# Seven block products for eight in a second place, and weight blocks loaded in twos

## The chip, the core and the metric

The kernel runs on one core of a Trainium2 chip. Its engines are TensorE (PE, matmuls), VectorE (DVE), ScalarE (ACT), GpSimd (POOL) and SyncE (SP); all work in order from their own queues and wait for one another by semaphores. SP issues nearly all DMAs, POOL the accumulating ones. The metric is device time in microseconds (us) of one execution, the median over the runs; 1468.02 us before (three runs, 1467.19 to 1469.15).

## The reference

A trunk of two layers for 512 tokens and 16 learned ones ahead of them (528 in all), 1024 features, all float32. Layer 0 is forgetting attention, layer 1 a gated linear recurrence (HGRN2); each is followed by a gated MLP with a causal depthwise convolution of three taps:

```python
def conv_ffn(h, norm_g, w_gate, w_up, conv_w, conv_b, w_down):
    xn = rms_norm(h, norm_g)
    a = xn @ w_gate
    L = a.shape[1]
    a_pad = jnp.pad(a, ((0, 0), (CONV_WIDTH - 1, 0), (0, 0)))
    a = (conv_b + conv_w[0] * a_pad[:, 0:L] + conv_w[1] * a_pad[:, 1:L + 1]
         + conv_w[2] * a_pad[:, 2:L + 2])
    return (jax.nn.silu(a) * (xn @ w_up)) @ w_down
```

The hidden width is 2816, that is 22 tiles of 128. The change is in the two MLPs and in what feeds them.

## The kernel before

Features lie on the partitions, tokens along the free dimension. Each product is made from three matmuls of rounded float32: a block is split into hi (its rounded value, a cast on ScalarE) and lo (the rest, a subtraction on VectorE), and hi·hi, hi·lo and lo·hi are summed in PSUM. So `weights` (L183) loads a raw block by SP, casts hi, subtracts lo; it has two raw, three hi and three lo buffers of 128 x 1024 (512 KB).

An MLP (`ffn`) goes through its 22 hidden tiles in runs. `RUNS = [(0, 6), (12, 5)]` names a run's first tile and r, its number of pairs. For each tile `hidden` multiplies gate and up weights with the tokens: 8 input blocks x 3 matmuls for each half or all of the tokens (layer 0: two halves of 264 for both; layer 1: 256 and 258 for the gate, 512 for up). VectorE and ScalarE do the convolution, the silu and the product in between.

The down-projection is done after each run, for two output tiles at a time (four pairs of output tiles, `mp`): a matrix of 2 x 2 blocks (two output tiles by two halves of the run) times one of 2 x 2 blocks (two halves of the run by two halves of the tokens), by Strassen's scheme in Winograd's form, seven block products of r blocks each instead of eight. Its left sides are three blocks of the weights themselves (w11, w12, w22) and four sums s1 to s4 of blocks. The right sides, seven "forms", are made on VectorE from each pair of hidden tiles and kept in `fhi` and `flo`. Four PSUM banks A, B, C, D take the products; two copies on ScalarE hand a partial sum on, and `put` adds results to the residual `h`.

The sums s1 to s4 are made in DRAM ahead of time by `sum_blocks`, a generator: a step is an SP copy into a DRAM tile and one or two accumulating DMAs of POOL. One step is taken behind most weight loads (`next(self.summing, None)`): those of layer 0 from the attention's output projection on, those of layer 1 during HGRN2. The seven left sides of a down-projection are loaded by `left` (L1128), seven transfers of 384 or 320 KB, into a pool of eight buffers (`temp`) which the hidden tiles use too, and split by `parts` (L1117) in the same three hi and lo buffers.

A scheduler in the build sets the order of each engine's instructions from the program's dependences and its own estimate of durations; the text's order does not bind it. The order of the loads on SP and of the products on TensorE near the down-projection is therefore shown with the change.

Of the kernel before, what the change touches and what calls it, by code (L numbers as in the profile page):

```python
# [21 lines left out]
P = 128  # L22
# [7 lines left out]
RUNS = [(0, 6), (12, 5)]  # L30
# [51 lines left out]
class Builder:  # L82
# [97 lines left out]
    def weights(self, src, n, w=P, parts=1):  # L180
# [13 lines left out]
        if parts == 1:  # L194
            self.load = nc.sync.dma_start(raw, src)
            next(self.summing, None)
            nc.scalar.copy(hi, raw)  # L197
            self.sub(lo, raw, hi.bitcast(F32))
            return u
# [3 lines left out]
    def sum_blocks(self, layer):  # L203

        nc = self.nc
        for mp, c0, r in [(mp, *run) for run in RUNS for mp in range(KT // 2)]:
            src = lambda m, half: self.a[f"dn{layer}"][2 * mp + m][:, (c0 + half * r) * P : (c0 + half * r + r) * P]
            s1, s2, s3, s4 = self.sums[layer, mp, c0] = [
                self.hbm.tile([P, r * P], F32, name=f"s{i}", tag=f"s{i}_{layer}_{mp}_{c0}") for i in range(1, 5)
            ]  # L210
            w11, w12, w21, w22 = src(0, 0), src(0, 1), src(1, 0), src(1, 1)
            for out, x, *rest in (s1, w21, w22), (s2, w21, w22, w11), (s3, w11, w21), (s4, w12, s2):
                self.after(nc.sync.dma_start(out, x), self.load)
                for y in rest:
                    nc.gpsimd.dma_start(out, y, accum_op=ALU.add, max_dma_last_dim=4 * r * P)  # L215
                yield 1
# [127 lines left out]
    def fox(self, ctx):  # L344
# [320 lines left out]
        self.summing = self.sum_blocks(0)  # L665
# [117 lines left out]
    def hgrn(self, ctx):  # L783
# [239 lines left out]
        for m in range(-3, KT):  # L1023
            if m == -2:
                self.summing = self.sum_blocks(1)
# [20 lines left out]
    def ffn(self, ctx, layer, a0, o0):  # L1046

        nc, a = self.nc, self.a
        ga, up = (halves(t0) if T - t0 > 512 else [(t0, T - t0)] for t0 in (a0, o0))
# [3 lines left out]
        self.normsplit(gcol, a0)  # L1053
        segs = (SEG0, SEG1)[layer]
        am, rs = self.token_stats(segs)
        self.spread_rs(rs, segs)
        def unit(w, toks, x):
            for t0, tn in toks:
                ps = self.anybank()[:, :tn]
# [4 lines left out]
        n = T - o0  # L1064
        hw = n // 2

        def hidden(m, early=None):

            A, t, s = (temp(w, nm) for w, nm in ((T + 2, "A"), (n, "t"), (n, "s")))
            if o0 == 0:  # L1070
                nc.gpsimd.memset(A[:, 0:2], 0.0)
            wg, wu = (self.weights(a[f"gu{layer}"][m, i], KT) for i in range(2))
            if early is not None:
                early()
            for ps, t0, tn in unit([wg], ga, self.x):
                nc.vector.tensor_tensor(A[:, 2 + t0 : 2 + t0 + tn], ps, self.rsb[:, t0 : t0 + tn], ALU.mult)
            c0 = cw + 3 * m
# [5 lines left out]
            self.act(s, t, AF.Silu)  # L1083
            nc.vector.tensor_tensor(t, s, self.rsb[:, o0:], ALU.mult)
            for ps, t0, tn in unit([wu], up, self.x):
                tv = t[:, t0 - o0 : t0 - o0 + tn]
                nc.vector.tensor_tensor(tv, ps, tv, ALU.mult)
            return t
# [4 lines left out]
        def put_form(f, j, x, fhi, flo):  # L1093
            x = x.rearrange("p (f t) -> p f t", t=hw)
            f = slice(f, f + x.shape[1])
            nc.scalar.copy(fhi[:, f, j, :], x)
            self.sub(flo[:, f, j, :], x, fhi[:, f, j, :].bitcast(F32))
# [194 lines left out]
```

## Time and profile before

| | |
|---|---|
| median of three runs | 1468.02 us (1467.19 to 1469.15) |
| the profiled execution | 1466.04 us, of it a span of 1464.3 us |
| TensorE busy | 1442.8 us (99%), granted clock 0.998 |
| VectorE, ScalarE busy | 961.5 us (66%), 627.8 us (43%) |
| bytes moved | 202.64 MB, mean 138 GB/s |
| first down-projections: layer 0, layer 1 | from about 529.8 us, from about 1235.7 us |

A row of the timeline gives start, duration, engine, line, operation, tiles and shape, and in brackets the idle time before it with what ended it. "SPq" and "PEq" are the sequencers. A row of windows gives, for a stretch, the busy time of each engine with its count of instructions, the granted clock, the share of the 16 DMA engines and GB/s; with one engine chosen, that engine alone. A row of waits gives total, count and longest. Matmuls overlap in the pipeline: their price is the distance of starts.

### The profile page before, as it was taken

To read this page: it belongs to the slowest core of one execution; us is meant where nothing else is said; L and a number is where in the kernel's file an instruction comes from. 1 tells how busy PE (TensorE), PEld (TensorE's weight loads), DVE (VectorE), ACT (ScalarE), POOL (GpSimd) and SP (SyncE) were. 2 spreads that over 40 slices of the span, in tenths; PEclk is the share of its full clock that TensorE was granted. 3 is DMA by queue.
4 is the path that set the end of the run, shared out by engine and by line. 5 is a ranking of instruction groups with operands and counts; after the bars stand their busy time and mean duration, and the time that the engine had idled before them with its cause. 6 is when DMAs were issued, how large, how long until landed. Compare 5 with 4: busy or idle time off the path is not lost.

```text
span 1464.3 us, 29095 instructions
## 1 busy us (share of the span) xinstructions
PE 1442.8 (99%) x11620; PEld 1358.6 (93%) x11620; DVE 961.5 (66%) x2083; ACT 627.8 (43%) x1206; POOL 101.3 (7%) x205
## 2 busy tenths in 40 slices
PE   7999999999999999999999999999999999999999
PEld 6888888988999999999999999999999998999999
DVE  7555555775567765667776667687566666657665
ACT  5355555663344344334562333333343334434343
POOL 6000000001112200000001101111000000000000
PEclk9999999999999999999999999999999999999999
DMA  4433335436989973322636827475532234622254
GB/s 160 119 105 90 94 99 129 124 87 166 288 213 239 231 214 115 101 88 102 191 94 159 213 62 188 137 174 132 129 102 87 87 101 155 191 76 98 94 166 137
DMA packets 75934, 202.64 MB, mean 138 GB/s; under 512 B 10888, under 2 KB 13448, under 8 KB 75800
## 3 DMA queue, kind: packets, MB, share of 16 engines
q1 hardware_dynamic: 64280, 171.95, 36.9%
q0 software_dynamic: 11520, 28.84, 12.3%
q8 instruction: 91, 1.49, 0.4%
q14 instruction: 43, 0.35, 0.1%
HBM read 185.31 MB, written 54.00 MB: 163 GB/s over the span
## 4 chain that ended last, share of the span: by engine, by line
PE 95%; DMA 1%; DVE 1%; ACT 1%; issue 1%; SPq 1%; DVEq 0%; ACTq 0%
PE psp L226 12%; PE psp L229 12%; PE psp L230 12%; PE pss L230 8%; PE pss L226 8%; PE pss L229 8%; PE psp L275 6%; PE psp L1151 3%; PE psp L1149 3%; PE psp L1150 3%; PE psc L760 2%; PE psd L1150 1%; PE psd L1151 1%; PE psd L1149 1%; PE pss L914 1%; PE pss L689 1%
## 5 line engine op out<-in xcount | busy, mean ns | idle before, releaser
L226 PE MATMUL psp<-xhi,hi 128*128 128x264 f32 (+3 forms) x1160 | 352.1, 304 | 5.9 <-ACT xhi L295 5.9
L229 PE MATMUL psp<-xlo,hi 128*128 128x264 f32 (+3 forms) x1160 | 352.8, 304 | 2.8 <-DVE xlo L296 2.8
L230 PE MATMUL psp<-xhi,lo 128*128 128x264 f32 (+3 forms) x1160 | 352.7, 304 | 0.0
L197 ACT CAST hi<-raw 128x1024 fp32r<-128x1024 f32 (+1 forms) x170 | 174.8, 1029 | 317.7 <-PE psp L229 114.9
L125 DVE TENSOR_TENSOR lo<-raw,hi 128x1024 fp32r<-128x1024 f32 (+1 forms) x174 | 208.4, 1199 | 75.2 <-ACT hi L197 71.4
L226 PEld LDWEIGHTS psp<-xhi,hi 128*128 128x128 f32 x1160 | 218.7, 189 | 17.4 <-ACT xhi L295 5.9
L230 PE MATMUL pss<-xhi,lo 128*128 128x264 f32 (+2 forms) x824 | 233.7, 284 | 0.0
L226 PE MATMUL pss<-xhi,hi 128*128 128x264 f32 (+2 forms) x824 | 233.1, 283 | 0.0
L229 PE MATMUL pss<-xlo,hi 128*128 128x264 f32 (+2 forms) x824 | 233.0, 283 | 0.0
L229 PEld LDWEIGHTS psp<-xlo,hi 128*128 128x128 f32 x1160 | 219.3, 189 | 13.2 <-DVE xlo L296 3.8
L230 PEld LDWEIGHTS psp<-xhi,lo 128*128 128x128 f32 x1160 | 219.5, 189 | 9.4 <-issue 1.6
L226 PEld LDWEIGHTS pss<-xhi,hi 128*128 128x128 f32 x824 | 155.3, 189 | 0.9
L229 PEld LDWEIGHTS pss<-xlo,hi 128*128 128x128 f32 x824 | 155.1, 188 | 0.9
L230 PEld LDWEIGHTS pss<-xhi,lo 128*128 128x128 f32 x824 | 154.9, 188 | 0.0
L1122 ACT CAST hi<-left 128x768 fp32r<-128x768 f32 (+1 forms) x112 | 86.8, 780 | 113.3 <-PE psp L1150 41.0
L125 DVE TENSOR_TENSOR lo<-left,hi 128x768 fp32r<-128x768 f32 (+1 forms) x112 | 99.2, 891 | 44.5 <-ACT hi L1122 44.3
L1149 PE MATMUL psp<-fhi,hi 128*128 128x264 f32 (+1 forms) x352 | 99.8, 284 | 0.1
L1151 PE MATMUL psp<-fhi,lo 128*128 128x264 f32 (+1 forms) x352 | 99.5, 283 | 0.0
L1150 PE MATMUL psp<-flo,hi 128*128 128x264 f32 (+1 forms) x352 | 99.4, 282 | 0.0
L215 POOL DMA_DIRECT2D s<-dn x64 | 54.0, 871 | 285.3 <-DMA s<-dn 264.5
L118 ACT ACTIVATE s<-t 128x528 f32<-128x528 f32 (+1 forms) x44 | 28.1, 639 | 98.8 <-DVE t L1082 98.8
L275 PE MATMUL psp<-hi,xhi 128*128 128x256 f32 x232 | 66.9, 288 | 2.7 <-ACT v L562 2.7
(423 smaller groups left out, 3023.2 us busy)
## 6 DMA issues: line engine op xcount, KB each, us to landing
raw<-gu SPq DMA_DIRECT2D x88, 512.0 KB
pk<-stg SPq DMA_DIRECT2D x48, 264.0 KB
s<-dn SPq DMA_DIRECT2D x32, 384.0 KB
s<-dn POOLq DMA_DIRECT2D x32, 384.0 KB, 7.0
left<-s SPq DMA_DIRECT2D x32, 384.0 KB
s<-dn SPq DMA_DIRECT2D x32, 320.0 KB
s<-dn POOLq DMA_DIRECT2D x32, 320.0 KB, 6.5
left<-s SPq DMA_DIRECT2D x32, 320.0 KB
```

What stands on the lines that cost most here:

```text
L125: self.nc.vector.tensor_tensor(out, x, y, ALU.subtract)
L197: nc.scalar.copy(hi, raw)
L215: nc.gpsimd.dma_start(out, y, accum_op=ALU.add, max_dma_last_dim=4 * r * P)
L226: ins = mm(ps, hi[:, i, :], xh, start=k == 0, stop=False)
L229: mm(ps, hi[:, i, :], xl, start=False, stop=False)
L230: mm(ps, lo[:, i, :], xh, start=False, stop=k == total - 1)
L275: mm(ps[:tn, :256], y[:, t0 : t0 + tn], w, start=n == 0, stop=n == 23)
L760: ins = mm(o, v[:kn, j, 2 * (p % 2) + hd, :], w[hd][0], start=j == 0, stop=j == last)
L1122: nc.scalar.copy(hi, raw)
L1149: mm(ps, hi[:, c], xh, start=start and k == 0, stop=False, skip_group_check=not start)
L1150: mm(ps, hi[:, c], xl, start=False, stop=False, skip_group_check=not start)
L1151: mm(ps, lo[:, c], xh, start=False, stop=k == r - 1, skip_group_check=not start)
```

## The change

- `RUNS` becomes three runs of 4, 4 and 3 pairs, in both MLPs.
- In the second MLP (layer 1), all pairs but the first two make their gate features in the seven-product form too: two hidden tiles at a time, the 1024 inputs as two halves of four blocks, the tokens as two halves of 258 (from token 12). The routine is shared by both uses (`seven`). Four of the seven right forms of the input are made once, in `xfhi` and `xflo`, beside the two plain pairs; their left sums are made in DRAM like the others, one generator (`all_sums`) for everything.
- A left side is loaded in twos: w11 and w12 in one transfer, s1 and s2 in one, s3 and s4 in one, then w22 alone; four transfers for seven. They go through `weights` and its two raw buffers; the eight `temp` buffers are gone.
- Gate tiles sit in one buffer `A` for two tiles; some forms are made two or four at a time.

```diff
@@ -27,7 +27,8 @@
...
-RUNS = [(0, 6), (12, 5)]
+RUNS = [(0, 4), (8, 4), (16, 3)]
+SEVEN = {1: 2}
@@ -177,7 +178,7 @@
...
-    def weights(self, src, n, w=P, parts=1):
+    def weights(self, src, n, w=P, parts=1, step=True):
@@ -193,27 +194,95 @@
...
             self.load = nc.sync.dma_start(raw, src)
-            next(self.summing, None)
+            if step:
+                next(self.summing, None)
             nc.scalar.copy(hi, raw)
             self.sub(lo, raw, hi.bitcast(F32))
             return u
         m = n * w // parts
...
-    def sum_blocks(self, layer):
+    def sum_blocks(self, key, r, w11, w12, w21, w22):
...
+        n = r * P
+        name = "s" + "_".join(map(str, key))
+        sums = [self.hbm.tile([P, 2 * n], F32, name=f"{name}_{i}", tag=f"{name}_{i}") for i in range(2)]
+        s1, s2, s3, s4 = (x[:, c : c + n] for x in sums for c in (0, n))
+        for out, x, *rest in (s1, w21, w22), (s2, w21, w22, w11), (s3, w11, w21), (s4, w12, s2):
+            self.after(nc.sync.dma_start(out, x), self.load)
+            for y in rest:
+                nc.gpsimd.dma_start(out, y, accum_op=ALU.add, max_dma_last_dim=4 * n)
+            if out is s4:
+                self.sums[key] = sums
+            yield 1
...
+    def all_sums(self):
+        for layer in range(2):
+            for i, (c0, r) in enumerate(RUNS if layer in SEVEN else ()):
+                for j in range(SEVEN[layer] if i == 0 else 0, r):
+                    yield from self.sum_blocks(("gate", layer, c0, j), 4, *self.gate_blocks(layer, c0, r, j))
+            for c0, r in RUNS:
+                for mp in range(KT // 2):
+                    yield from self.sum_blocks(("down", layer, c0, mp), r, *self.down_blocks(layer, mp, c0, r))
+    def left(self, key, r, blocks, whole):
+        def get(i):
+            while key not in self.sums:
+                next(self.summing)
+            src = (whole, *self.sums[key], blocks[3])[i]
+            return self.weights(src, r if i == 3 else 2 * r, step=i == 0)
+        return get
+    def seven(self, get, right, r, w, put, first=()):
...
+        A, D = (self.bank("p")[:, :w] for _ in range(2))
+        B, C = (self.bank(x)[:, :w] for x in "cd")
+        def product(ps, unit, k0, f, start):
+            hi, lo, _ = unit
+            for k in range(r):
+                xh, xl = right(f, k)
+                mm(ps, hi[:, k0 + k, :], xh, start=start and k == 0, stop=False, skip_group_check=not start)
+                mm(ps, hi[:, k0 + k, :], xl, start=False, stop=False, skip_group_check=not start)
+                mm(ps, lo[:, k0 + k, :], xh, start=False, stop=k == r - 1, skip_group_check=not start)
+        first = list(first)
+        unit = lambda i: first.pop(0) if first else get(i)
+        w1 = unit(0)
+        product(A, w1, 0, 0, True)
+        nc.scalar.copy(B, A)
+        s12 = unit(1)
+        product(D, s12, 0, 3, True)
+        put(1, 1, D, False)
+        product(B, s12, r, 4, False)
+        nc.scalar.copy(C, B)
+        put(0, 1, B, False)
+        product(A, w1, r, 1, False)
+        put(0, 0, A, True)
+        s34 = get(2)
+        product(C, s34, 0, 5, False)
+        put(1, 1, C, True)
+        product(D, s34, r, 2, False)
+        put(0, 1, D, True)
+        product(C, get(3), 0, 6, False)
+        put(1, 0, C, True)
@@ -662,7 +731,7 @@
...
-        self.summing = self.sum_blocks(0)
+        self.summing = self.all_sums()
@@ -1021,8 +1090,6 @@
...
-            if m == -2:
-                self.summing = self.sum_blocks(1)
@@ -1046,150 +1113,169 @@
     def ffn(self, ctx, layer, a0, o0):
...
+        split = layer in SEVEN
+        g0 = a0 // 4 * 4 if split else a0
+        gw = (T - g0) // 2
...
-                ps = self.anybank()[:, :tn]
+                ps = (self.bank("s") if split else self.anybank())[:, :tn]
...
-        def hidden(m, early=None):
-            A, t, s = (temp(w, nm) for w, nm in ((T + 2, "A"), (n, "t"), (n, "s")))
-            if o0 == 0:
-                nc.gpsimd.memset(A[:, 0:2], 0.0)
-            wg, wu = (self.weights(a[f"gu{layer}"][m, i], KT) for i in range(2))
...
+        if split:
+            xfhi, xflo = (sp.tile([P, 4, 4, gw], F32R, name=nm) for nm in ("xfhi", "xflo"))
+        def input_forms(k):
+            u = blocks(gw)
+            for x, kt in ((u[:, 0:8:7, :], k), (u[:, 1:3, :], 4 + k)):
+                h = self.h[:, kt, g0:].rearrange("p (f t) -> p f t", t=gw)
+                nc.scalar.activation(x, h, AF.Copy, scale=self.vcol(gcol + kt))
+            differences(u)
+            put_form(0, 4, k, u[:, 3:7, :], xfhi, xflo)
...
+        def input_form(f, k):
+            if f >= 3:
+                return xfhi[:, f - 3, k, :], xflo[:, f - 3, k, :]
+            k, t0 = ((k, g0), (4 + k, g0), (4 + k, g0 + gw))[f]
+            return tuple(y[:, t0 : t0 + gw] for y in self.x[k])
...
+        def gates(As, c0, r, j):
+            def put(m, half, ps, last):
+                t0 = g0 + half * gw
+                out = As[:, m, 2 + t0 : 2 + t0 + gw]
+                if half and last:
+                    nc.vector.tensor_tensor(out, out, ps, ALU.subtract if m else ALU.add)
+                else:
+                    nc.scalar.activation(out, ps, AF.Copy, scale=-1.0 if m else 1.0)
+                if last and half != m:
+                    x = As[:, m, 2 + g0 : 2 + T]
+                    nc.vector.tensor_tensor(x, x, self.rsb[:, g0:], ALU.mult)
+            get = self.left(
+                ("gate", layer, c0, j), 4, self.gate_blocks(layer, c0, r, j), a[f"gu{layer}"][c0 + j, 0]
+            )
+            self.seven(get, input_form, 4, gw, put)
+        def hidden(out, A, m, early=None):
...
+            wu = self.weights(a[f"gu{layer}"][m, 1], KT)
+            if early is not None:
+                early()
...
-        def temp(w, name):
-            return s2.tile([P, 6 * P], F32, name=name, tag="temp", bufs=8)[:, :w]
...
-        def forms(j, c0, r, fhi, flo, early):
-            form = lambda f, x: put_form(f, j, x, fhi, flo)
-            t1 = hidden(c0 + j)
-            x11, x12 = t1[:, :hw], t1[:, hw:]
-            ta, tb = temp(n, "ta"), temp(n, "tb")
-            self.sub(ta[:, :hw], x11, x12)
-            form(0, x11)
-            form(3, ta[:, :hw])
-            t2 = hidden(c0 + r + j, early)
...
-            form(1, t2)
...
-        def left(mp, c0, r, i):
-            raw = temp(r * P, "left")
-            if isinstance(i, int):
-                src = self.sums[layer, mp, c0][i - 1]
+                f = (t0 - o0) // hw
+                tv = out[:, f : f + tn // hw, :]
+                nc.vector.tensor_tensor(tv, two(ps), tv, ALU.mult)
+        def forms(j, c0, r, fhi, flo, plain, early):
...
+            As = s2.tile([P, 2, T + 2], F32, name="A", tag="A", bufs=1)
+            if o0 == 0:
+                nc.gpsimd.memset(As[:, :, 0:2], 0.0)
+            u = blocks(hw)
+            for i in range(2):
+                m = c0 + i * r + j
+                if plain:
+                    gate(As[:, i, :], m)
+                elif i == 0:
+                    gates(As, c0, r, j)
+                hidden(u[:, 1:3, :] if i else u[:, 0:8:7, :], As[:, i, :], m, early if i else None)
+                if plain and split:
+                    input_forms(2 * j + i)
+            form = lambda f, n: put_form(f, n, j, u[:, f : f + n, :], fhi, flo)
...
+            differences(u)
+            if early is None:
+                form(1, 2)
+                form(3, 4)
...
-                k0 = (c0 + i[1] * r) * P
-                src = a[f"dn{layer}"][2 * mp + i[0]][:, k0 : k0 + r * P]
-            nc.sync.dma_start(raw, src)
-            return parts(raw)
-        def down(mp, c0, r, fhi, flo, last, first):
...
+                for f, k in ((3, 2), (1, 1), (5, 1), (2, 1), (6, 1)):
+                    form(f, k)
+        def down(mp, c0, r, fhi, flo, last, get, first):
...
-            A, D = (self.bank("p")[:, :hw] for _ in range(2))
-            B, C = (self.bank(x)[:, :hw] for x in "cd")
-            ws = lambda i: left(mp, c0, r, i)
-            product(A, first[0] if first else ws((0, 0)), 0, True)
-            nc.scalar.copy(B, A)
-            product(D, first[1] if first else ws(1), 3, True)
-            put(1, 1, D, ALU.subtract)
-            product(B, ws(2), 4, False)
...
-            product(A, ws((0, 1)), 1, False)
-            put(0, 0, A, ALU.add, True)
-            product(C, ws(3), 5, False)
-            put(1, 1, C, ALU.subtract, True)
-            product(D, ws(4), 2, False)
-            put(0, 1, D, ALU.add, True)
-            product(C, ws((1, 1)), 6, False)
-            put(1, 0, C, ALU.subtract, True)
+            self.seven(get, lambda f, k: (fhi[:, f, k, :], flo[:, f, k, :]), r, hw, put, first)
...
-        for c0, r in RUNS:
-            fhi, flo = (sp.tile([P, 7, 6, hw], F32R, name=nm, tag=nm)[:, :, :r, :] for nm in ("fhi", "flo"))
...
+            fhi, flo = (sp.tile([P, 7, 4, hw], F32R, name=nm, tag=nm)[:, :, :r, :] for nm in ("fhi", "flo"))
+            get = []
+            for mp in range(KT // 2):
+                whole = a[f"dn{layer}"][2 * mp][:, c0 * P : (c0 + 2 * r) * P]
+                get.append(self.left(("down", layer, c0, mp), r, self.down_blocks(layer, mp, c0, r), whole))
             first = []
             for j in range(r):
-                early = None if j < r - 1 else lambda: first.append([left(0, c0, r, i) for i in ((0, 0), 1)])
-                forms(j, c0, r, fhi, flo, early)
+                early = None if j < r - 1 else lambda: first.extend(get[0](x) for x in range(2))
+                plain = not split or i == 0 and j < SEVEN[layer]
+                forms(j, c0, r, fhi, flo, plain, early)
             for mp in range(KT // 2):
-                down(mp, c0, r, fhi, flo, c0 > 0, first.pop() if first else None)
+                down(mp, c0, r, fhi, flo, c0 + 2 * r == NF, get[mp], first if mp == 0 else ())
```

In the order, on SP in the second down-projection of layer 1's first run before (left: a weight block or a sum s, on its way to SBUF):

```order
L1135 DMA left<-dn 128x768 [waits DMAHW0_49,DVE_49]
L1135 DMA left<-s_10409 128x768 [waits DMAHW1_49,DMASW7_49,DVE_49]
L1135 DMA left<-s_10410 128x768 [waits DMAHW2_49,DMASW1_49,DVE_49]
L1135 DMA left<-dn 128x768 [waits DMAHW3_49,DVE_49]
L1135 DMA left<-dn 128x768 [waits DMAHW4_49,DVE_49]
```

and now, in layer 1's second run (sdown_8_1_0 holds s1 and s2, sdown_8_1_1 s3 and s4 of one pair of output tiles):

```order
L196 DMA raw<-dn 128x1024 [waits DMAHW6_49,DVE_49]
L196 DMA raw<-sdown_8_1_0_13767 128x1024 [waits DMASW4_49,DMAHW7_49,DMASW2_49,DVE_49]
L196 DMA raw<-sdown_8_1_1_13768 128x1024 [waits DMASW6_49,DMAHW0_49,DMASW5_49,DVE_49]
L196 DMA raw<-dn 128x512 [waits DMAHW1_49,DVE_49]
L196 DMA raw<-dn 128x1024 [waits DMAHW2_49,DVE_49]
```

Four loads stand where seven stood, and they go to the raw buffers; each waits for VectorE, which has to be done with the load two places ahead.

On TensorE, where one pair of output tiles hands over to the next in layer 1's first run, the first rows of the products now (hi_14736 is s3 and s4, hi_14768 w22 of the one pair; hi_14791 is w11 and w12, hi_14812 s1 and s2, hi_14858 s3 and s4 of the next):

```order
L262 MATMUL psp_14786<-fhi_13759,hi_14791 128x256 [waits Activation_49]
...
L262 MATMUL psd_14681<-fhi_13759,hi_14736 128x256 [waits Activation_49]
...
L264 MATMUL psp_14786<-fhi_13759,lo_14792 128x256 [waits DVE_49]
...
L262 MATMUL psd_14681<-fhi_13759,hi_14768 128x256 [waits DVE_49]
...
L262 MATMUL psp_14787<-fhi_13759,hi_14812 128x256 [waits Activation_49]
L262 MATMUL psc_14788<-fhi_13759,hi_14812 128x256 [waits Activation_49]
...
L262 MATMUL psp_14787<-fhi_13759,hi_14858 128x256 [waits DVE_49,Activation_49]
```

The next pair's first product (psp_14786) stands ahead of the last product of this one (w22, into psd_14681), its other product with the same load follows behind, then those with s1, s2 and with s3, s4.

More of the change, by code (lines that the diff above doesn't have):

```diff
@@ L201, in weights @@
         return *u, [partial(load, slice(i * m, i * m + m)) for i in range(parts)]
-    def sum_blocks(self, layer):
+    def sum_blocks(self, key, r, w11, w12, w21, w22):
         nc = self.nc
[L206 to L216, printed above, removed]
+        n = r * P
[9 more added lines that the diff above has]
+            yield 1
@@ L1138, in down @@
-        def down(mp, c0, r, fhi, flo, last, first):
-            def product(ps, w, f, start):
-                hi, lo = w
-                mm = nc.tensor.matmul
-                for k in range(r):
-                    c = slice(k * P, k * P + P)
-                    xh, xl = fhi[:, f, k, :], flo[:, f, k, :]
-                    mm(ps, hi[:, c], xh, start=start and k == 0, stop=False, skip_group_check=not start)
-                    mm(ps, hi[:, c], xl, start=False, stop=False, skip_group_check=not start)
-                    mm(ps, lo[:, c], xh, start=False, stop=k == r - 1, skip_group_check=not start)
-            def put(m, half, ps, op, store=False):
+                f = (t0 - o0) // hw
```

68 lines of the change are left out of this document (37 added, 31 removed).

## The prediction

> **What bounds the kernel now.** I read the page first, then what TensorE waits for, then the stages one by one.
>
> ```profile
> PE 1442.8 (99%) x11620; PEld 1358.6 (93%) x11620; DVE 961.5 (66%) x2083; ACT 627.8 (43%) x1206; POOL 101.3 (7%) x205
> PE 95%; DMA 1%; DVE 1%; ACT 1%; issue 1%; SPq 1%; DVEq 0%; ACTq 0%
> PE psp L226 <- ACT xhi L295: 5.9, 1, 5.9
> PE psc L1151 <- DVE lo L125: 2.0, 3, 0.9
> ```
>
> TensorE is busy 99% of the span and 95% of the chain that ended last is its own work. Of its few waits the largest is at the start; in the down-projections it waits 2.0 us in all. So a matmul that goes is worth its own time, and every wait put into TensorE's stream is paid in full.
>
> The matmuls are pipelined, so I price them by starts, not by durations. In the second MLP:
>
> ```profile
> 1122.48 0.28 PE L226 MATMUL pss<-xhi,hi 128*128 128x256 f32 x1
> 1128.21 0.40 PE L226 MATMUL psp<-xhi,hi 128*128 128x512 f32 x1
> 1133.79 0.29 PE L226 MATMUL pss<-xhi,hi 128*128 128x256 f32 x1
> 1246.00:1294.00 48.00, 48.00 (x407) 1.00 0.44 135
> 532.00:592.00 60.00, 60.00 (x494) 1.00 0.49 154
> ```
>
> A gate tile (48 matmuls of 256 or 258 columns) takes 1128.21 - 1122.48 = 5.73 us, 0.119 us each; the up tile behind it 5.58 us. The last two rows are windows inside the down-projections of layers 1 and 0: gap-free, and less two matmuls cut by the edges 48/405 = 0.1185 us and 60/492 = 0.122 us for one matmul.
>
> **The matmuls that go.** Nine of the eleven pairs of the second MLP get the seven-product form: 7 products of 4 blocks of 3 matmuls are 84, for 96 before. 12 x 9 = 108 fewer. A pair's gate takes 84 x 0.119 = 10.0 us for 11.46, so 9 x 1.43 = **-12.9 us**. The down-projections keep their count: 7 x 3 x 11 x 4 in each layer, in three runs as in two.
>
> **The loads of the down-projection.** Before, the block products are fed through eight "left" buffers. The row below says what ScalarE's casts wait for there: a finished product (a free hi buffer), not a transfer.
>
> ```profile
> ACT hi L1122 <- PE psp L1150: 41.0, 41, 1.4
> 1256.19 0.84 ACT L1122 CAST hi<-left 128x768 fp32r<-128x768 f32 x1 [1.03 <-PE psp L1150]
> 1257.05 0.96 DVE L125 TENSOR_TENSOR lo<-left,hi 128x768 fp32r<-128x768 f32 x1 [0.33 <-ACT hi L1122]
> ```
>
> The change takes those eight away and sends every block through the two "raw" buffers. A raw buffer is free when VectorE has made lo from it; then SP issues the next load. In the order, loads alternate between the two, four to a pair of output tiles: w1, s12, s34, w22. So the first buffer always carries w1 and s34, two full blocks, and the time of a pair of output tiles cannot be below two turns of that buffer. The trace has such turns, after each down-projection, where the raw buffers start up with SP free:
>
> ```profile
> 1293.82 1.23 DVE L125 TENSOR_TENSOR lo<-raw,hi 128x1024 fp32r<-128x1024 f32 x1 [0.54 <-ACT hi L197]
> 1295.07 2.23 SPq L195 DMA_DIRECT2D raw<-gu  x2
> 1298.61 1.05 ACT L197 CAST hi<-raw 128x1024 fp32r<-128x1024 f32 x1 [2.93 <-DMA raw<-gu]
> 1299.70 1.23 DVE L125 TENSOR_TENSOR lo<-raw,hi 128x1024 fp32r<-128x1024 f32 x1 [2.39 <-ACT hi L197]
> 589.52 0.33 SPq L195 DMA_DIRECT2D raw<-gu  x1
> 592.80 1.05 ACT L197 CAST hi<-raw 128x1024 fp32r<-128x1024 f32 x1 [2.60 <-DMA raw<-gu]
> 593.88 1.23 DVE L125 TENSOR_TENSOR lo<-raw,hi 128x1024 fp32r<-128x1024 f32 x1 [1.99 <-ACT hi L197]
> ```
>
> VectorE ends at 1295.05, SP issues at 1295.07, the cast starts at 1298.61 (3.54 us later), lo is done at 1300.93: a turn of 5.86 us. The other is 595.11 - 589.52 = 5.59. I take 5.7, two turns 11.4 us.
>
> TensorE needs 84 x 0.1185 = 9.95 us for a pair of output tiles in layer 1 and 10.25 in layer 0, where r is 4. So each hand-over to the next pair waits 11.4 - 9.95 = 1.45 us, or 1.15. With r = 3 a load is 384 KB: cast to end of lo is 0.86 + 0.96 = 1.82; the landing lies between three quarters of 3.41 (the mean of the two) and all of it, I take 3.0: a turn of 4.8, two 9.6, against 63 x 0.1185 = 7.5 and 7.7. Wait 2.1 or 1.9.
>
> The order shows the first product of the next pair (w1) ahead of the last of this one (w22), and TensorE runs in order: it stands at that product though w22 may be there. On ScalarE the casts stand in the order of the loads, on SP the next loads behind the waiting one; all slip together, so the wait recurs at each hand-over. Of a run's four hand-overs the first is covered, since two units are loaded during the last up-projection; behind the last run there is no fourth. Layer 0: 6 x 1.15 + 3 x 1.9 = 12.6. Layer 1: 6 x 1.45 + 2 x 2.1 = 12.9. Together **+25.5 us**. The ends: a turn of 5.59 and a landing at three quarters give about 19; 5.86 and a full landing about 34.
>
> The Trainium skill has a price for a transfer (DMA: Bandwidth & Descriptors, section "Anatomy of one DMA"): about 2.0 us plus the bytes at 436 GB/s, fitted for GpSimd's path. By it 512 KB take 3.2 us, the turn would be 5.5 and this term about 21; the measured landing, on SP's path, is a little longer and decides.
>
> **The sums beside them.** Block sums are made in DRAM, one step (an SP copy, then one or two accumulating DMAs of POOL) at most weight loads. Steps go from 64 to 132: 48 for each layer's downs, 36 for the gates. They now run on into the down-projections, one step to a pair of output tiles, in all three runs of layer 0 and the first of layer 1. What a step does to raw turns stands in the stage before the first MLP, where each load has one of 384 KB behind it:
>
> ```profile
> 371.93 0.33 SPq L195 DMA_DIRECT2D raw<-gu  x1
> 377.69 0.33 SPq L195 DMA_DIRECT2D raw<-gu  x1
> 382.35 0.33 SPq L195 DMA_DIRECT2D raw<-gu  x1
> 386.37 0.33 SPq L195 DMA_DIRECT2D raw<-gu  x1
> 391.20 0.33 SPq L195 DMA_DIRECT2D raw<-gu  x1
> 397.57 0.33 SPq L195 DMA_DIRECT2D raw<-gu  x1
> 365.00:405.00 40.00, 39.80 (x329) 39.59 (x328) 23.82 (x46) 15.14 (x19) 6.65 (x9) 1.00 0.99 284
> ```
>
> Every second load uses the same buffer: turns of 10.4, 8.7, 8.9 and 11.2 us, mean 9.8, with the DMA engines 99% busy. That is 4.1 over 5.7, for two steps; two thirds of 2.05 is 1.4 us for a step of 256 KB. It costs nothing where the step meets only the other buffer. The DMA share in down-projections is 0.44 without steps, so I take the full 1.4: 4 runs x 3 hand-overs x 1.4 = **+17 us**, ends 0 and, at twice that, 34.
>
> **The rest.** Six starts of a down-projection for four: the four cost at most the 2.0 us above, so +1. The forms of the input are made on ScalarE and VectorE beside two plain pairs (45 us of TensorE). In a seven-product pair VectorE gets 1.5 more blocks to split and longer evictions:
>
> ```profile
> 1119.00:1230.00 111.00, 111.00 (x711) 100.70 (x710) 78.28 (x129) 44.60 (x65) 0.00 (x0) 1.00 0.30 98
> ```
>
> VectorE's 78.28 of 111 us are 16 us in a pair of tiles; plus 1.5 x 1.2 and 0.5 make 18 of the pair's 21.2 us. It hides, but without much room. In layer 0 the conv's zero columns are set by POOL, once a pair, in a buffer that is now single, behind accumulating DMAs. These three I bound by 0 and 12 us and take +4.
>
> **Sum.** 1464.3 - 12.9 + 25.5 + 17 + 5 = 1498.9 us span. The profiled execution was 1466.0 with a span of 1464.3, and 2.0 below the median of 1468.0; with both the forecast is 1503 us, slower by 2.4%.
>
> **Rivals.** (1) The loads stay hidden and the gain remains. For it: three loads fewer for each pair of output tiles, and three hi/lo buffers that let the splitting run ahead. The Trainium skill backs this (DMA: Bandwidth & Descriptors, section "Rules for kernel authors"): gather many small transfers into a large one. By that the change would be right; no run here shows it for blocks of this size. Time: 1468 - 12.9 + 1 = 1456. Against it: the turns above hold for a single load of 512 KB. Chance 0.12.
>
> (2) The turns bind only where r is 3 and TensorE needs just 7.5 us: 3 x 1.9 + 2 x 2.1 and 3 for the rest are 13, which the gates give back: 1468, no change. For it: the three hi/lo buffers let a late block be split ahead of its product. Against it: with r = 4 a turn would have to be under 5.0 us, and none above is under 5.59. Chance 0.05.
>
> (3) The gates of the second MLP bind as well. A pair there needs six loads, three turns of each buffer: 3 x 5.7 = 17.1 us in 21.2, which fits; but with two steps to a pair, at the turns of 9.8, 29 us. Six pairs run while steps are left: up to 6 x 8 = 48 more, 1551. Against it: the steps there are of two thirds and one half the size. Chance 0.09 for ends above 1535.
>
> (4) The clock falls. Page and windows show a granted clock of 1.00 with gaps under 1 us. If 3.4 us at half speed followed each of the 17 hand-overs, 17 x 1.7 = 29: 1532. The Trainium skill (TensorE: Matmul & The Clock Gate, "What's actually happening") halves the clock after an idle window of about 3.4 us; by that rule my waits of 1 to 3.5 us are mostly too short, and the trace has none that tests it in this stage. Chance 0.02.
>
> **How the numbers follow.** The forecast has 0.72, between 1478 and 1535. Rival 1 has 0.12, rival 2 0.05, 3 and 4 together 0.11. The range, 1466 to 1535, leaves out rival 1 and the far end of 3, 0.19 in all. A measurement tells 0.2% here, 2.9 us: faster 0.13 (rival 1 and a little of 2), same 0.04, slower 0.83.
>
> **What would show it.** In the changed profile TensorE's waits on hi and lo of the weight split should come to 35 to 50 us, nearly all at hand-overs inside down-projections, 1 to 3.5 us each, longest where r is 3 or steps run; there ScalarE's casts should wait for a DMA, and SP for VectorE's lo. Gate stretches of the second MLP should take 10.0 us a pair. I am wrong if the casts in the down-projections still wait for products, or if the waits sit in the gates.

## The result

| | before | changed |
|---|---|---|
| median | 1467.6 us (1464.4 to 1469.2) | 1525.9 us (1524.4 to 1527.3) |
| profiled span | 1464.3 us | 1522.6 us |
| ratio | | 1.040 (95%: 1.038 to 1.042) |

The change makes the kernel slower by 4.0%. The page of the changed kernel (busy times, then the chain that ended last), and some of what TensorE and ScalarE's casts wait for in the whole span (total, count, longest):

```profile
PE 1456.9 (96%) x11512; PEld 1358.4 (89%) x11512; DVE 998.1 (66%) x2101; ACT 666.9 (44%) x1264; POOL 168.9 (11%) x279
PE 79%; DMA 10%; DVE 5%; ACT 4%; issue 2%; SPq 1%; ACTq 0%; DVEq 0%
PE psp L262 <- DVE h L1253: 10.6, 12, 1.6
PE psp L262 <- ACT hi L199: 10.5, 11, 1.9
PE psp L264 <- DVE lo L126: 8.0, 13, 0.8
ACT hi L199 <- DMA raw<-sdown: 39.3, 23, 3.4
ACT hi L199 <- DMA raw<-dn: 32.5, 19, 4.8
```

108 matmuls fewer, and yet TensorE is busy 14 us longer and its share falls from 99% to 96%. In the chain, TensorE's share falls from 95% to 79% and the DMA's rises from 1% to 10%. The casts of the down-projections' weights now wait for transfers of weights (dn) and sums (sdown) too; before, they waited for a product.

The turn of a raw buffer, in the second down-projection of layer 1, where no sum step runs. Rows of the timeline, the loads of one raw buffer alone (w1, then s3 and s4, then the next w1), and the product that stands for the first lo:

```profile
1385.71 1.05 ACT L199 CAST hi<-raw 128x1024 fp32r<-128x1024 f32 x1 [1.27 <-DMA raw<-dn]
1386.79 1.22 DVE L126 TENSOR_TENSOR lo<-raw,hi 128x1024 fp32r<-128x1024 f32 x1 [0.72 <-ACT hi L199]
1388.05 0.33 SPq L196 DMA_DIRECT2D raw<-sdown  x1
1388.07 0.39 PE L264 MATMUL psp<-fhi,lo 128*128 128x256 f32 x1 [0.76 <-DVE lo L126]
1391.40 1.05 ACT L199 CAST hi<-raw 128x1024 fp32r<-128x1024 f32 x1 [1.48 <-DMA raw<-sdown]
1392.49 1.23 DVE L126 TENSOR_TENSOR lo<-raw,hi 128x1024 fp32r<-128x1024 f32 x1 [0.79 <-ACT hi L199]
1393.74 0.33 SPq L196 DMA_DIRECT2D raw<-dn  x1
1397.22 1.05 ACT L199 CAST hi<-raw 128x1024 fp32r<-128x1024 f32 x1 [2.56 <-DMA raw<-dn]
1398.30 1.22 DVE L126 TENSOR_TENSOR lo<-raw,hi 128x1024 fp32r<-128x1024 f32 x1 [1.14 <-ACT hi L199]
```

VectorE ends lo at 1388.01 and SP issues at 1388.05; lo of that load ends at 1393.72, SP issues at 1393.74; the next lo ends at 1399.52. Turns of 5.71 and 5.80 us, and 11.5 us from one w1 to the next (1385.71 to 1397.22), where the products of a pair of output tiles take 9.95. From issue to cast are 3.35 and 3.48 us. The Trainium skill (DMA: Bandwidth & Descriptors, "Anatomy of one DMA") would give an estimated 3.2 us for 512 KB on GpSimd's path; on SP's path here it is a little more.

**Where the 58 us are.** I took the distance of each matmul's start to the next, less its usual pitch, in the two MLPs of the changed kernel, and sorted what is over (us):

| | layer 0 | layer 1 | both |
|---|---|---|---|
| hand-overs inside down-projections | 23.1 | 13.8 | 36.8 |
| the first pair of output tiles of each run | 4.8 | 8.8 | 13.7 |
| gates of layer 1 and the up tiles behind them | | 10.2 | 10.2 |
| first loads behind a down-projection | 4.9 | | 4.9 |
| matmuls at half clock | 2.3 | 4.4 | 6.7 |

These are 72.3 us; the kernel before has 5.2 of the same kinds. With the gates' saving (12.4, below) and 3.6 us outside the MLPs: 72.3 - 5.2 - 12.4 + 3.6 = 58.3, the difference of the spans.

The seven-product gates do what they should once they run: the first matmul of a gate pair, twice in a row.

```profile
1321.53 0.28 PE L262 MATMUL psp<-xhi,hi 128*128 128x258 f32 x1
1342.77 0.28 PE L262 MATMUL psp<-xhi,hi 128*128 128x258 f32 x1
```

A pair of tiles takes 21.24 us. Before it was 2 x (5.73 + 5.58) = 22.62, so 1.38 us a pair and 12.4 for nine.

The first down-projection of layer 1's second run waits three times within 3 us, for the forms of the run's last pair (fhi, flo) and for a PSUM bank that VectorE frees:

```profile
1369.73 0.39 PE L262 MATMUL psp<-fhi,hi 128*128 128x256 f32 x1 [0.48 <-ACT fhi L1140]
1371.02 0.39 PE L263 MATMUL psp<-flo,hi 128*128 128x256 f32 x1 [0.78 <-DVE flo L126]
1372.29 0.39 PE L262 MATMUL psp<-fhi,hi 128*128 128x256 f32 x1 [0.53 <-DVE h L1253]
```

And the gates wait too: the first of them for the forms of the input, and the up tile behind the first gate of the third run for its weights (hi, lo), which come late through the same two raw buffers:

```profile
1188.57 0.39 PE L262 MATMUL psp<-xfhi,hi 128*128 128x258 f32 x1 [1.82 <-ACT xfhi L1140]
1189.84 0.39 PE L263 MATMUL psp<-xflo,hi 128*128 128x258 f32 x1 [0.77 <-DVE xflo L126]
1422.10 0.50 PE L295 MATMUL pss<-xhi,hi 128*128 128x512 f32 x1 [1.09 <-ACT hi L199]
1423.36 0.50 PE L299 MATMUL pss<-xhi,lo 128*128 128x512 f32 x1 [0.53 <-DVE lo L126]
```

### The profile page after: what moved, and what is told of

Same layout as the page of the kernel before. It is cut to its first block, busy times and chain, and to the rows that moved or that the text cites. A ratio compares the mean times of both kernels' runs of the same rounds, so it can differ in the third digit from the quotient of the medians.

```text
span 1522.6 us, 29168 instructions
## 1 busy us (share of the span) xinstructions
PE 1456.9 (96%) x11512; PEld 1358.4 (89%) x11512; DVE 998.1 (66%) x2101; ACT 666.9 (44%) x1264; POOL 168.9 (11%) x279
## 4 chain that ended last, share of the span: by engine, by line
PE 79%; DMA 10%; DVE 5%; ACT 4%; issue 2%; SPq 1%; ACTq 0%; DVEq 0%
PE psp L295 9%; PE psp L299 9%; PE psp L298 8%; PE pss L299 8%; PE pss L295 8%; PE pss L298 8%; PE psp L344 5%; ACT hi L199 3%; DMA raw<-dn 3%; DVE lo L126 3%; DMA raw<-sdown 3%; PE psc L829 2%; PE psp L262 2%; PE psp L264 2%; PE psp L263 2%
## 5 line engine op out<-in xcount | busy, mean ns | idle before, releaser
L199 ACT CAST hi<-raw 128x1024 fp32r<-128x1024 f32 (+3 forms) x284 | 273.8, 966 | 466.7 <-PE psp L298 101.6
L126 DVE TENSOR_TENSOR lo<-raw,hi 128x1024 fp32r<-128x1024 f32 (+3 forms) x288 | 322.6, 1121 | 167.8 <-ACT hi L199 162.2
L295 PE MATMUL psp<-xhi,hi 128*128 128x264 f32 (+1 forms) x984 | 284.1, 290 | 6.3 <-ACT xhi L364 6.3
L298 PE MATMUL psp<-xlo,hi 128*128 128x264 f32 (+1 forms) x984 | 283.7, 289 | 3.3 <-DVE xlo L365 3.3
L299 PE MATMUL psp<-xhi,lo 128*128 128x264 f32 (+1 forms) x984 | 284.0, 289 | 0.5 <-DVE lo L126 0.5
L299 PEld LDWEIGHTS psp<-xhi,lo 128*128 128x128 f32 x984 | 187.2, 190 | 2.5 <-issue 1.6
L215 POOL DMA_DIRECT2D sdown<-dn x96 | 79.7, 857 | 451.6 <-DMA sdown<-dn 442.5
L262 PE MATMUL psp<-fhi,hi 128*128 128x264 f32 (+1 forms) x352 | 103.6, 295 | 22.7 <-DVE h L1253 10.6
L262 PEld LDWEIGHTS psp<-fhi,hi 128*128 128x128 f32 x352 | 67.4, 192 | 28.7 <-ACT hi L199 12.8
L264 PEld LDWEIGHTS psp<-fhi,lo 128*128 128x128 f32 x352 | 66.5, 191 | 9.5 <-DVE lo L126 9.5
L263 PEld LDWEIGHTS psp<-flo,hi 128*128 128x128 f32 x352 | 67.5, 192 | 4.2 <-DVE flo L126 4.0
```

The lines of the kernel that those rows point to most:

```text
L126: self.nc.vector.tensor_tensor(out, x, y, ALU.subtract)
L262: mm(ps, hi[:, k0 + k, :], xh, start=start and k == 0, stop=False, skip_group_check=not start)
L263: mm(ps, hi[:, k0 + k, :], xl, start=False, stop=False, skip_group_check=not start)
L264: mm(ps, lo[:, k0 + k, :], xh, start=False, stop=k == r - 1, skip_group_check=not start)
L295: ins = mm(ps, hi[:, i, :], xh, start=k == 0, stop=False)
L298: mm(ps, hi[:, i, :], xl, start=False, stop=False)
```

## The experiments

All are timed against the kernel before, whose median on these chips was 1466.6 to 1467.5 us. The changed kernel is at 1525.9.

**1. w22 in a buffer of its own.** One buffer of 256 KB for the fourth load of a pair of output tiles; nothing else.

```diff
+        own = self.pool(f"own_{layer}", 1, ctx=ctx)
...
-            return self.weights(src, r if i == 3 else 2 * r, step=i == 0)
+            return self.weights(src, r if i == 3 else 2 * r, step=i == 0, pool=pool if i == 3 else None)
```

> The changed kernel, with w22 (the fourth load of a pair of output tiles) in a buffer of its own of 256 KB; the three full loads alternate between the two raw buffers, so each turns 1.5 times a pair, not twice. Theory (turns of the raw buffers bind at the hand-overs): 1.5 x 5.7 = 8.6 us is under the 9.95 of TensorE, and with r = 3 1.5 x 4.8 = 7.2 under 7.5; the waits at hand-overs go, which are some 40 us by the trace of the changed kernel (its waits in down-projections less those at the starts of runs): 1485 us, between 1475 and 1497. Rival (PSUM banks: the next pair's first product waits for VectorE's put, not for a weight): less than 10 us gained, 1516 or more. Rival (the sum steps hold up every load): 10 to 20 gained, 1506 to 1516.

Measured: 1491.6 us, ratio 1.016 (1.014 to 1.019). 34 us gained. What ScalarE's casts out of the raw buffers waited for in the second run of layer 1, first in the changed kernel (a stretch of 40 us; total, count), then with w22 apart:

```profile
  DMA raw<-sdown: 5.6, 4
  DMA raw<-dn: 5.2, 3
  PE psd L263: 5.1, 2
  PE psc L263: 3.7, 3
```

```profile
  PE psd L263: 7.3, 5
  PE psc L263: 6.3, 4
  DMA raw<-sdown: 1.3, 1
```

The casts wait for products again and hardly for transfers. TensorE's waits on hi and lo fall from the 10.5 and 8.0 us shown above to 0.8 and 0.5, and by the distances of starts what the pairs of output tiles behind the first of each run lose falls from some 37 us to some 10. The theory of the turns holds, and the rival of the banks falls as the main cause. The waits that end with VectorE's put (h) stay, though: 8.7 us for 10.6. Run 10 shows for layer 0 that most of them go with more buffers; what holds the others is open.

**2. No sum steps.**

```diff
-            while key not in self.sums:
-                next(self.summing)
-            src = (whole, *self.sums[key], blocks[3])[i]
+            src = (whole, whole, whole, blocks[3])[i]
...
-        self.summing = self.all_sums()
+        self.summing = iter(())
```

> The changed kernel without the 132 sum steps: the loads of s1, s2 and s3, s4 fetch w11, w12 instead, so the copies and accumulating DMAs are gone while every load, cast and product stays; the sums of blocks are left out of the computation. Theory: the steps cost what the trace's comparison of runs with and without steps says, about 4 us in layer 0's first run and 3 in its last, and a little in the gates: 5 to 17 gained, 1509 to 1521. Rival (the steps' transfers are the main cause of the late loads): 30 or more gained, 1496 or less.

Measured: 1510.0 us, ratio 1.029 (1.027 to 1.031). 16 us gained, within the theory's 5 to 17, not the rival's 30. By the distances of starts, the down-projections of layer 0 take 13.3 us less, 2.3 of it because the matmuls at half clock do not occur there in this run; those of layer 1 gain nothing.

**3. Plain gates.**

```diff
-SEVEN = {1: 2}
+SEVEN = {}
```

> The changed kernel with no seven-product gates: all gates of the second MLP plain, 108 matmuls more, 36 sum steps and the forms of the input gone; three runs and loads in twos stay. Theory: the 12.9 us of the matmuls come back, and the waits that the trace shows in and around the seven-product gates (8.5 us) go, with a few us of steps: 1522 to 1532. Rival (the matmuls that went were worth their full time): 1538. Rival (the gates cost more than they save): under 1518.

Measured: 1518.2 us, ratio 1.035 (1.033 to 1.037). This is 7.8 us less than with the seven-product gates. Theory missed (1522 to 1532), the rival by which they cost more than they save is at its edge. What I had left out: they also burden the down-projections of their own layer. Those wait 16.5 us in this run (three runs, by the distances of starts) and 22.6 with the gates (13.8 + 8.8 above); their starts alone 1.2 us each in the first two runs for 2.3. By which path was not tested.

**4. The kernel before with three runs.**

```diff
-RUNS = [(0, 6), (12, 5)]
+RUNS = [(0, 4), (8, 4), (16, 3)]
...
-                down(mp, c0, r, fhi, flo, c0 > 0, first.pop() if first else None)
+                down(mp, c0, r, fhi, flo, c0 + 2 * r == NF, first.pop() if first else None)
```

> The kernel before with three runs of 4, 4 and 3 pairs and nothing else changed: seven loads through eight left buffers. Theory: two more starts of a down-projection and shorter products, but no raw turns: 2 to 8 us slower than before, 1470 to 1476. Rival (short runs themselves cost the time, since each start waits for the forms of the last pair and each load serves fewer matmuls): 1490 or more.

Measured: 1475.0 us, ratio 1.006 (1.004 to 1.008): 8.4 us slower, at the upper end of the theory. Short runs alone are about a seventh of the loss.

**5. Halves.** The cast and the subtraction of a full left side in two pieces each.

```diff
-            nc.scalar.copy(hi, raw)
-            self.sub(lo, raw, hi.bitcast(F32))
+            m = n * w // split
+            for c in (slice(i, i + m) for i in range(0, n * w, m)):
+                nc.scalar.copy(hi[:, c], raw[:, c])
+                self.sub(lo[:, c], raw[:, c], hi[:, c].bitcast(F32))
```

> The changed kernel, with the cast and the subtraction of each full load of a left side made in two halves, nothing else: the raw buffer is free after half a cast and half a subtraction behind the landing, some 3.5 + 0.62 + 0.69 = 4.8 us for the turn in place of 5.7. Theory (turns bind): two turns are 9.6 us, under the 9.95 of TensorE with r = 4, and some 8.1 against 7.5 with r = 3; most waits at hand-overs go: 20 to 32 us gained, 1494 to 1506. Rival (the number of loads through two buffers binds by the landing alone, or the two engines' queues are full): under 8 us gained, 1518 or more.

Measured: 1523.6 us, ratio 1.038 (1.037 to 1.040): nothing gained that can be told. The expectation was wrongly worked out, and the trace of this run shows it (a cast in two pieces, then VectorE, at one load):

```profile
1386.96 1.14 ACT L201 CAST hi<-raw 128x512 fp32r<-128x512 f32 x2 [1.41 <-DMA raw<-dn]
1387.62 0.69 DVE L126 TENSOR_TENSOR lo<-raw,hi 128x512 fp32r<-128x512 f32 x1 [0.95 <-ACT hi L201]
1388.22 0.41 DVE L1255 TENSOR_TENSOR h<-h,psp 128x256 f32<-128x256 f32 x1
1388.56 0.69 DVE L126 TENSOR_TENSOR lo<-raw,hi 128x512 fp32r<-128x512 f32 x1
```

The buffer is free only when both halves are done: from the start of the cast to the end of the second lo 1389.25 - 1386.96 = 2.29 us, where undivided it was 1388.01 - 1385.71 = 2.30, since a put came between the halves. So it is at three of the ten full loads of this down-projection; at the other seven it is 1.95 us, 0.35 less, where 0.9 less was expected. Two turns still do not fit into 9.95 us: w1 follows w1 after 11.5 us (1386.96 to 1398.48), as without halves, and the run hardly tests the theory.

**6. Early forms.** Forms 0 and 3 behind the first tile of a pair, as before the change.

```diff
+                if i == 0:
+                    self.sub(u[:, 3, :], u[:, 0, :], u[:, 7, :])
+                    form(0, 1)
+                    form(3, 1)
-            form(0, 1)
-            differences(u)
+            self.sub(u[:, 5, :], u[:, 2, :], u[:, 7, :])
...
```

> The changed kernel, with forms 0 and 3 of the hidden tiles made behind the first tile of a pair, as before the change, and the fused difference and the fused split of forms undone for that. Theory: the waits at the starts of down-projections in layer 1 (2.3, 2.3 and 3.2 us by the trace) come from these forms, and the lowered clock behind two of them too: 4 to 10 us gained, 1516 to 1522. Rival (those starts wait for the weights or the banks): less than 3 us.

Measured: 1523.3 us, ratio 1.039 (1.037 to 1.041): 2.6 us, the rival's size. But the starts did get better: by the distances of starts the first pairs of output tiles lose 6.3 us for 13.7, summed over both layers. The waits of TensorE from the start of the second run of layer 1 up to its third pair of output tiles:

```profile
1369.59 0.39 PE L262 MATMUL psp<-fhi,hi 128*128 128x256 f32 x1 [1.02 <-ACT hi L199]
1379.38 0.36 PE L262 MATMUL psp<-fhi,hi 128*128 128x256 f32 x1 [0.85 <-DVE h L1258]
1383.36 0.39 PE L262 MATMUL psp<-fhi,hi 128*128 128x256 f32 x1 [0.89 <-ACT hi L199]
```

One wait stands where three stood. But the second pair of output tiles then waits at 1379.38, where the changed kernel did not, and at the hand-over to the third (1383.36) 0.89 us for 0.76. In both MLPs together, by the distances of starts, the waits come to some 64 us for 68, and what is lost at half clock to 11 us for 7. So the late forms do cost time at the starts. The loads set the pace: TensorE begins earlier and waits later (its waits on hi rise from 10.5 to 15.0 us), and the clock takes back the rest.

**9. w22 apart and early forms together**, to test that reading (the edits of 1 and 6).

> The changed kernel with w22 in a buffer of its own and with the early forms, both alone known: 34 us gained and 3 gained. Theory (with two raw buffers the loads set the pace of a down-projection, so time won at its start is lost again at the next hand-over; with w22 apart TensorE sets the pace and the start counts): 6 to 12 us under the run with w22 apart, 1480 to 1486. Rival (the two are independent): 2 to 4 under it, 1488.

Measured: 1483.0 us, ratio 1.011 (1.009 to 1.012): 8.6 us under the first run by medians, 5.2 by the spans of the profiles (1488.7 and 1483.5). The time is the theory's, but the traces do not bear its reason out. The first pairs of output tiles lose 6 us for 12 in the first run, the later ones 15 for 10: the time won at the starts is lost again here too. The waits in the two MLPs come to some 40 us in both runs, and those on hi rise again (0.8 to 4.7); what differs is the time lost at half clock, 2.2 us for 6.6. The granted clock of the four executions was 0.993 to 0.997, in the first run 0.990 to 0.994. That early forms are worth more once w22 is apart is therefore not shown, and the rival is not ruled out: its 1488 is 5 us off, of which the clock can be 4.

**10. Four raw buffers for the first MLP's down-projections alone.**

```diff
+        own = None if split else self.pool(f"own_{layer}", 4, ctx=ctx)
...
-            return self.weights(src, r if i == 3 else 2 * r, step=i == 0)
+            return self.weights(src, r if i == 3 else 2 * r, step=i == 0, pool=pool)
```

> The changed kernel with four raw buffers of their own for the down-projections of the first MLP alone; the second MLP as changed, its two raw buffers too. Theory (turns, and the sum steps only as they lengthen turns): in the first MLP the hand-over waits go, steps or not, 20 to 28 us, and nothing in the second: 1498 to 1506. Rival (the steps keep the DMA engines full, however many buffers there are): 13 or less, the part that the run without sums got there: 1513 or more.

Measured: 1498.9 us, ratio 1.021 (1.020 to 1.023): 27 us gained. What the products waited for from the first down-projection of layer 0 to the end of the last: in the changed kernel, without sum steps (where the line numbers are two less), and here.

```profile
PE psp L262 <- ACT hi L199: 7.4, 7, 1.9
PE psp L262 <- DVE h L1253: 7.2, 6, 1.6
PE psp L264 <- DVE lo L126: 3.2, 6, 0.8
```

```profile
PE psp L262 <- DVE lo L126: 4.2, 7, 0.8
PE psp L260 <- ACT hi L199: 3.2, 6, 1.0
PE psp L260 <- DVE h L1251: 2.2, 2, 1.1
```

```profile
PE psp L262 <- DVE h L1254: 2.2, 2, 1.1
PE psp L262 <- ACT hi L199: 0.8, 1, 0.8
PE psp L264 <- DVE lo L126: 0.3, 1, 0.3
```

With four buffers most of the waits are gone with all steps in place; the two that end with a put (2.2 us) are left. So the steps' 13 us in layer 0 are no cost of their own: their transfers make the turns longer, and with buffers enough hardly anything waits for a turn.

**7 and 8. All mends, then in the second MLP alone.** Run 7: w22 apart, halves, early forms, and three plain pairs ahead of the seven-product gates (`SEVEN = {1: 3}`). Run 8: the same for layer 1, with the first MLP of the kernel before (two runs, eight left buffers; the sums of the second are made during it).

> The changed kernel with w22 in a buffer of its own, halves, early forms, and three plain pairs ahead of the seven-product gates instead of two, so that the forms of the input are ready when the first of them starts. Theory (each wait has its own cause, and they add): 1491.6 of the first run less 5 to 8 at the starts, 3 at the first gate (its 4.7 of waits and lowered clock against 1.4 of matmuls), 3 to 6 at the short runs: 1474 to 1482. Rival (waits move on to the next late thing): 1486 or more.

> The same mends for the second MLP, while the first MLP is the one of the kernel before: runs of 6 and 5 pairs, seven loads through eight left buffers. Theory (the first MLP got only the costs of the change: 15 us left in the first run of this study, a few less with the mends): 10 to 15 us under the run with all mends, 1460 to 1470; faster than before only if the second MLP keeps less than 11 us of waits. Rival (the sums of the second MLP, now made during the first, or its loads slow it again): 1472 or more.

Measured: 1474.0 us, ratio 1.006 (1.004 to 1.008), and 1464.8 us, ratio 0.999 (0.998 to 1.000). Both times lie where the theory put them; the distance, 9.2 us, is a little under its 10 to 15. What the change did to the first MLP was loss: no matmul goes there.

**11 and 12. A version under both kernels.** Run 11 is run 8 with w22 of the gates too in the buffer of its own; run 12 is run 11 with `RUNS = [(0, 3), (6, 4), (14, 4)]` in the second MLP.

> The run with the change in the second MLP alone and all mends, and w22 of the gates too in the buffer of its own. Theory: the up weights behind a gate get a raw buffer sooner, and the waits there (0.9 + 0.7 us by the trace) go: 1462 to 1464. Rival: no difference, 1465.

> The same with runs of 3, 4 and 4 pairs in the second MLP, so that the short run is the one with plain gates. Theory: the last down-projection, with 84 products for each pair of output tiles, is hidden better (4.7 us of excess in the short run by the trace, 1.4 in the others), but the first would take the short one's place: 1460 to 1466. Rival: the sums of the last run come too late, 1470.

Measured: 1462.2 us, ratio 0.997 (0.996 to 0.998), and 1465.1 us, ratio 0.999 (0.998 to 1.000). Both lie in their ranges; the other order of runs (12) gains nothing. Run 11 beats both kernels: 0.3% under the one before, 4% under the changed one. Its busy times and the largest wait in its second MLP:

```profile
PE 1437.3 (98%) x11524; PEld 1350.7 (92%) x11524; DVE 997.3 (68%) x2189; ACT 668.8 (46%) x1340; POOL 150.0 (10%) x265
PE psp L265 <- ACT hi L202: 2.5, 5, 0.6
```

Eight pairs of seven-product gates save 8 x 1.38 = 11 us, of which the median shows 5; about 7 us of waits more than before stay in that MLP by the distances of starts.

## Why the prediction was right, step by step

The direction and the mechanism held, and 1526 lies in 1466 to 1535. The forecast of 1503 was 23 us short: of the 58 us about 37 came from the mechanism that was forecast, 34 from terms that were priced at 5, and the matmuls gave back 12. That the range still held the time is owed to its width; in that part it was luck.

- **The matmuls that go**: -12.9 forecast, -12.4 measured.
- **Turns and sum steps**: 25.5 + 17 = 42.5 forecast, 36.8 measured at the hand-overs. The turn was taken at 5.7 us and measures 5.71 and 5.80. The steps were priced at 17 and come to 16 when taken out, but the step that spread them over both layers (1.4 us at each of 12 hand-overs, three of them in layer 1) was off: they cost 13 in layer 0's down-projections and nothing in layer 1's. The turns alone were well sized: without steps (run 2) the pairs behind the first lose some 13 us in layer 0 and 14 in layer 1, where 12.6 and 12.9 were forecast. But the prediction added turns and steps as if each had a price; run 10 shows one cause.
- **The rest**: +5 forecast, 33.9 measured (13.7 + 10.2 + 4.9 + 6.7 + 3.6 less the 5.2 of before). This step failed: "Six starts of a down-projection for four: the four cost at most the 2.0 us above, so +1". I took the price of a start from a kernel that makes forms 0 and 3 behind the first tile of a pair. The change fuses the forms and makes all of them behind the second tile, which stood in the diff; the first pairs of output tiles cost 13.7 us, where the four of the kernel before cost 3.6 by the same measure. The fusing is only part of that: three runs alone bring it to 8.5 (run 4, forms early), fused forms behind plain gates 9.4 (run 3), and the last 4 us come only where seven-product gates stand ahead of them. For the gates and the input forms I took +4 within 0 to 12; they measure 10.2, and 4.9 more behind the down-projections of layer 0, where the next stage's first loads pass the same two buffers.
- **Rival 1**, the loads stay hidden, was wrong here. The Trainium skill's rule that backed it (DMA: Bandwidth & Descriptors, "Rules for kernel authors": coalesce) speaks of small transfers; these were 320 and 384 KB already. What the larger ones cost was the wait for a free buffer: with the same transfers and more buffers, runs 1 and 10 gained 34 and 27 us.
- **Rival 2**, waits only where r is 3, falls: runs with r = 4 wait at their hand-overs too, as the one in the rows above, where TensorE stands 0.76 us for lo at 1388.07.
- **Rival 3**, the gates bind as well, was half right: they do wait, and run 3 shows that they cost more than they save in this kernel, but nowhere by the 8 us a pair that it priced.
- **Rival 4**, the clock, happened at four places in the two MLPs, 6.7 us, not at all 17.
- **The signs**: waits on hi and lo of the weight split were to be 35 to 50 us; the rows above show 18.5, none over 1.9, and another 10.6 that ends with VectorE's put. Only the distances of starts give the 36.8. The casts did come to wait for DMAs, though in the rows of run 1 nearly half of the time that they wait in the changed kernel still ends with a product. The waits in the gates, named as a sign of being wrong, were a side of it, 10.2 us, not the main one.
- **The chances**: rival 1 (0.12) and the ends of rival 3 above 1535 (0.09) leave 0.21 outside the range as they are stated, not 0.19.

## What to carry to other kernels

Merging loads is paid in buffers: what counts is how often the busiest buffer must turn (issue, landing, cast, subtraction) within one round of the consumer. Here two turns of 5.75 us, longer while sums were made, stood against 9.95 of work, and one more buffer of 256 KB brought 34 us back. Time won at one place can be lost at the next (early forms: 7 us at the starts, 2.6 in all), and a difference of a few us between two runs can be the clock's: look at the granted clock and the sum of the waits before you give it a cause. And when a change fuses small instructions, look for who waits for the first piece: its price at a boundary cannot be taken from the kernel that made the pieces apart.

## What was not expected of the hardware

The clock of TensorE fell though TensorE was never idle for long. Windows of 3.3 or 3.4 us around three places in layer 1 of the changed kernel, then one behind which the clock stayed (TensorE's busy time and count, then the granted clock):

```profile
1369.20:1372.60 3.40, 1.61 (x9) 1.00 0.09 12
1372.60:1376.00 3.40, 3.40 (x18) 0.50 0.70 219
1420.40:1423.80 3.40, 1.78 (x9) 1.00 0.41 157
1423.80:1427.10 3.30, 3.30 (x10) 0.50 0.65 209
1188.50:1191.80 3.30, 2.23 (x13) 0.98 0.85 263
1191.80:1195.10 3.30, 3.30 (x16) 0.50 0.68 155
1260.50:1263.90 3.40, 2.01 (x15) 1.00 0.90 301
```

The longest single wait at these places is 1.82 us, but TensorE was busy only 1.61, 1.78 and 2.23 us of 3.3 or 3.4, and for the next 3.4 us it ran at half clock, at about 1.5 us each. The busy time of the records alone does not tell where the clock falls: behind the last window, with 2.01 us, less than the 2.23 of the third place, it stayed. The Trainium skill (TensorE: Matmul & The Clock Gate, "What's actually happening") puts the fall behind an idle window of about 3.4 us; the length agrees, but here windows that were busy for 47 to 68% of the time were enough. Where the bound lies was not tested.
